# SSD scan slots put into one fixed TensorE order, decay tables built without TensorE, transposes of a tile kept together

## The chip, the cores and the metric

The kernel runs on one core of a Trainium2 chip. The metric is the device time of one launch in microseconds (us). PE is TensorE, DVE is VectorE, ACT is ScalarE, POOL is GpSimd; SP issues nearly all DMAs.

## The reference

Two layers act on 1024 latent tokens and 256 context tokens of width 1024: windowed attention, then a bidirectional Mamba-2 (SSD) mixer, then a final norm. The change lies in the SSD layer, which has 8 groups of 4 heads and cuts the sequence into chunks of 128 tokens:

```python
xbc = jax.nn.silu(centred_depthwise_conv(xbc, conv_w, conv_b))
...
a_cs = jnp.cumsum(da, axis=2)
decay_to_end = jnp.exp(a_last[:, :, None] - a_cs)
states = jnp.einsum('bcsgn,bcsgr,bcsgrp->bcgrpn', bm, decay_to_end, xdt)
...
lmat = jnp.exp(jnp.where(lower, diff, -jnp.inf))
cb = jnp.einsum('bcqgn,bcsgn->bcqsg', cm, bm)
y_diag = jnp.einsum('bcqsg,bcqsgr,bcsgrp->bcqgrp', cb, lmat, xdt)
y_off = jnp.einsum('bcqgn,bcgrpn,bcqgr->bcqgrp', cm, h_prev, jnp.exp(a_cs))
```

Here `diff[q, s] = a_cs[q] - a_cs[s]`. A forward and a backward pass both start from states that the context leaves. The sum of both is gated with `silu(z)`, normalised per group and multiplied by `w_out`.

## The kernel before

All weights and activations of the projections are split into a high and a low fp32r part, and each product is three matmuls (`wh*uH`, `wh*uL`, `wl*uH`).

**Front.** `front` computes for one group, as a generator that yields after each matmul: four tiles of 128 channels (`bT`, two halves of x in `cacc`, `cT`) and the gate `z`. A latent tile is 48 matmuls of 512 columns (L1069) into `pj2` (two buffers); for `bT` and the x halves 24 matmuls of 256 columns (L1060) into `psD` (one buffer) come first for the context. What follows a tile is put into a queue (`Queue`) of small steps: on ACT the conv's middle tap (L982), on DVE four taps (L986), on ACT a tanh (L993), on DVE the silu (L994), then transposes on PE (L1033) back into the same PSUM tile and copies on ACT (L1036). Steps given with a delay come out when so much PE cost has been yielded (`LATE`).

**Chain.** `states` makes, for each group, 11 steps that carry the states through the context and backward through the latent chunks: `xweight` on POOL (L1144), one matmul into `psD` (L1167), `decay` on POOL (L1149), an add on DVE (L1179).

**Slots.** 64 slots, one for each group and chunk (`slot`), each with: scores `pcb` (L1215), the two inter-chunk products `po` (L1217, L1218), the forward state `S` (L1224), the masked diagonal product `yd` (L1244, against the table `M`), and for the slot before two transposes of the finished row (L1272). `M` is exp of a difference of two rows, made by `decays` in two halves: DMAs bring rows of the cumulative sums, ACT casts them (L1195), four fp32r matmuls with one-hot rows spread them over 128 partitions (L1203), DVE takes the backward half where the mask `before` says so (L1204), ACT applies exp (L1205). All these PSUM tiles share the tag `psX` with three buffers. While the slots of group g run, `fill` draws front matmuls of group g+1 (in the last group: matmuls of the output projection, L1484) between them.

**What sets the order.** The code gives a priority order; a scheduler then reorders the instructions of each engine, PE's among them, by what its own model finds ready. Each engine executes its own list in order. Before the slots, `ssd_consts` computes dt, the cumulative sums and their exponentials for all groups (L914 to L976), beside the front of group 0.

Of the kernel before, what the change touches and what calls it, by code (L numbers as in the profile page):

```python
# [17 lines left out]
P = 128  # L18
D = 1024
KT = D // P  # L20
LAT = 1024
# [24 lines left out]
    cacc=2, cctx=1, bT=2, cT=2, xn4=4, xn2=1, bn4=4, bn2=1, sz=2, xw=2, hf=2, hx=2, M=2, y2=1, xs=1, uT=2, pj2=2, psX=3, sk=2, dg=2,  # L46
# [13 lines left out]
LATE = 3.0  # L60
SEGS = (1.5, 2.0, 2.0, 2.2, 2.2)
# [3 lines left out]
class Queue:  # L65
# [10 lines left out]
    def pop(self):  # L76
        if not self.q:
            self.late.popleft()[1]()
            return
        f = self.q.popleft()  # L80
        if isinstance(f, tuple):
            self.late.extend((self.now + f[0], x) for x in f[1])
        else:
            f()
# [19 lines left out]
class Kernel:  # L104
# [758 lines left out]
    def ssd_consts(self, p):  # L863
# [18 lines left out]
        self.dtb = t(p, [P, NCH, 32], F32, "dtb")  # L882
        self.eal = t(p, [P, 64, NT], F32, "eal")

        self.acs_d = t(dr, [2, 64, LAT], F32, "acs")
        self.v_d = t(dr, [2, 64, LAT], F32, "vrow")
# [28 lines left out]
        for lo, n, chunks in ((0, 768, (0, 1, 2, 3, 8, 9)), (768, 512, (4, 5, 6, 7))):  # L915
# [24 lines left out]
            def rows(dst, src):  # L940
                h = t(q, [64, 512], F32R, "rowh", 2)
                l = t(q, [64, 512], F32R, "rowl", 2)
                nc.scalar.copy(h, src[:, :512])
                nc.vector.tensor_sub(l, src[:, :512], h)
                for x, y in enumerate((h, l)):
                    nc.sync.dma_start(dst[x, :, chunks[0] * P : chunks[0] * P + 512], y.bitcast(F32))

            rows(self.acs_d, acs)
# [11 lines left out]
            rows(self.v_d, ln)  # L960
# [6 lines left out]
            for b, c in enumerate(chunks):  # L967
# [4 lines left out]
                if c < NCH:  # L972
# [3 lines left out]
                    nc.scalar.copy(self.dtb[:, c, :], pt[:, 160:192])  # L976
        nc.sync.dma_start(self.eal, eal_d.broadcast_to([P, 64, NT]))
# [12 lines left out]
    def silu(self, raw, acc):  # L990
# [3 lines left out]
                lambda: nc.vector.scalar_tensor_tensor(acc, in0=raw, scalar=1.0, in1=acc, op0=ALU.add, op1=ALU.mult)]  # L994

    def front(self, g, st, post, first=None):
# [31 lines left out]
        def natural(raw, acc, dst, o, n):  # L1028
# [12 lines left out]
            return [(LATE, steps)]  # L1041
# [9 lines left out]
        for n, (x, kind) in enumerate(tiles):  # L1051
# [4 lines left out]
            if nat:  # L1056
                raw = t(ps, [P, 512], F32, "psD")[:, :CTX]
                for k in range(KT):
                    for y, (l, r) in enumerate(((wh, uH), (wh, uL), (wl, uH))):
                        nc.tensor.matmul(raw, l[:, k, :], r[2][:, k, :], start=k + y == 0, stop=k == KT - 1 and y == 2)  # L1060
                        yield N256
                acc = t(pf, [P, CTX], F32, "cctx")
                post.extend(self.taps(x, raw, acc, 0, CTX, CTX) + self.silu(raw, acc) + natural(raw, acc, [(st[nat[0]][2], 0, 2)], nat[1], 2))
# [16 lines left out]
            post.append((LATE, [done]) if nat else done)  # L1080
        need(w)
# [28 lines left out]
    def ssd(self, c0):  # L1110
# [11 lines left out]
        rraw = t(ps2, [32, 6, P], F32, "rraw")  # L1122
        rrow = t(ps2, [P, 6, P], F32R, "rrow")
        nc.sync.dma_start(rraw, a["rrow"].rearrange("p (r n) -> p r n", r=6))
        nc.vector.memset(rrow.bitcast(F32), 0.0)
# [60 lines left out]
        def load_rows(n):  # L1186
            g, c = divmod(n, NCH)
            cs = slice(c * P, (c + 1) * P)
            ar = self.acs_d.rearrange("h (d k) n -> (h d) k n", d=2)[:, 4 * g : 4 * g + 4, cs]
            nc.sync.dma_start(rraw[0:4, :4], ar)  # L1190
            for d in range(2):
                nc.sync.dma_start(rraw[4 + 8 * d : 12 + 8 * d, 4 + d], self.v_d[:, hd(d, g), cs])

        def round_rows(n):
            nc.scalar.copy(rrow[:32], rraw)  # L1195
            if n + 1 < G * NCH:
                load_rows(n + 1)

# [437 lines left out]
```

## Time and profile before

| | us |
|---|---|
| runs | 1855.55, 1860.01, 1861.53; median 1860.01 |
| the profiled execution | 1855.31, of which span 1853.6 |
| SSD slots, first scores to the last diagonal product (starts) | 868.1 to 1752.7 |
| PE busy | 1779.0 of the span |
| DVE / ACT / POOL busy | 1172.0 / 898.8 / 730.7 |

A matmul's row gives a start and a modelled end, and ends overlap the next start; what a matmul costs PE is read from one start to the next.

### The profile page before, as it was taken

The numbers are of one execution on the slowest core, as the hardware profiler recorded it, in microseconds if no ns is written. First come the engines' busy times: TensorE is split into PE (matmuls) and PEld (weight loads), VectorE is DVE, ScalarE is ACT, GpSimd is POOL, SyncE is SP. The second block draws the span as 40 slices with busy tenths as digits, with TensorE's granted clock in tenths as the row PEclk, the third lists the DMA queues.
The fourth block names the chain that finished last, engine by engine and source line by source line (L and its number), as shares of the span: only waits on it lengthen the run. The fifth ranks groups of instructions, "written<-read, shape, count | busy, mean of one in ns | idle before, by whom it ended". The sixth has DMA issues, their size and how long they took to land. (4 is left out here: it accounts for less than half of the span.)

```text
span 1853.6 us, 29612 instructions
## 1 busy us (share of the span) xinstructions
PE 1779.0 (96%) x10628; PEld 1531.0 (83%) x10628; DVE 1172.0 (63%) x2208; ACT 898.8 (48%) x1852; POOL 730.7 (39%) x1007
## 2 busy tenths in 40 slices
PE   6999999999999899879999999999999999999997
PEld 4797767788898787668898898989889898988886
DVE  3654437877778666773766657576665756754743
ACT  3521236777788664652444435344443534543532
POOL 2441137654466465003352443525344352542411
PEclk9999999999999999889999999999999999999998
DMA  8767866443354435121111111111111111433552
GB/s 295 279 168 239 286 166 153 116 107 97 91 135 123 131 122 188 61 64 35 31 46 45 35 46 34 47 33 39 53 34 47 34 48 33 152 114 97 178 162 71
DMA packets 145491, 196.30 MB, mean 106 GB/s; under 512 B 15392, under 2 KB 84896, under 8 KB 144320
## 3 DMA queue, kind: packets, MB, share of 16 engines
q1 hardware_dynamic: 111280, 175.76, 29.6%
q0 software_dynamic: 34064, 18.65, 5.5%
q8 instruction: 84, 1.38, 0.3%
q14 instruction: 63, 0.52, 0.1%
HBM read 158.73 MB, written 35.92 MB: 105 GB/s over the span
## 5 line engine op out<-in xcount | busy, mean ns | idle before, releaser
L222 PE MATMUL pj<-uH,wh 128*128 128x256 f32 (+1 forms) x652 | 232.8, 357 | 7.6 <-DVE rope_b L531 2.3
L224 PE MATMUL pj<-uH,wl 128*128 128x256 f32 (+1 forms) x652 | 219.2, 336 | 0.0
L223 PE MATMUL pj<-uL,wh 128*128 128x256 f32 (+1 forms) x652 | 219.2, 336 | 0.0
L1144 POOL TENSOR_TENSOR xw<-xn,dtdec 128x256 f32<-128x256 f32 x144 | 106.4, 741 | 210.4 <-PE psD L1167 103.1
L1069 PE MATMUL pj<-uH,wh 128*128 128x512 f32 x512 | 172.1, 406 | 1.2 <-ACT xn L1036 1.2
L1069 PE MATMUL pj<-uH,wl 128*128 128x512 f32 x512 | 171.6, 404 | 0.0
L1069 PE MATMUL pj<-uL,wh 128*128 128x512 f32 x512 | 168.2, 398 | 0.0
L210 POOL TENSOR_TENSOR wl<-wr,wh 128x512 fp32r<-128x512 f32 x92 | 121.6, 1325 | 98.3 <-ACT wh L208 97.2
L1094 PE MATMUL pj<-wh,uH 128*128 128x256 f32 x512 | 154.7, 302 | 0.0
L698 DVE TENSOR_TENSOR pl<-pt,ph 128x512 fp32r<-128x512 f32 x168 | 114.3, 688 | 60.7 <-ACT ph L697 59.9
L222 PEld LDWEIGHTS pj<-uH,wh 128*128 128x128 f32 x652 | 123.9, 190 | 34.2 <-issue 7.8
L1094 PE MATMUL pj<-wh,uL 128*128 128x256 f32 x512 | 151.2, 295 | 0.0
L1094 PE MATMUL pj<-wl,uH 128*128 128x256 f32 x512 | 150.8, 295 | 0.0
L1273 ACT ACTIVATE uT<-psX,nw 128x128 f32<-128x128 f32 x128 | 46.9, 367 | 190.1 <-PE psX L1272 189.0
L224 PEld LDWEIGHTS pj<-uH,wl 128*128 128x128 f32 x652 | 123.6, 190 | 14.8 <-issue 1.7
L672 DVE CUSTOM_DVE_ANT_0 sm<-S,mask,nsink 128x640 f32<-128x640 f32 (+2 forms) x160 | 118.8, 772 | 24.6 <-PE S L669 12.2
L208 ACT CAST wh<-wr 128x512 fp32r<-128x512 f32 (+1 forms) x132 | 84.8, 645 | 101.3 <-PE pj L223 74.2
L223 PEld LDWEIGHTS pj<-uL,wh 128*128 128x128 f32 x652 | 124.2, 191 | 11.5 <-issue 2.8
L697 ACT CAST ph<-pt 128x512 fp32r<-128x512 f32 x168 | 97.4, 585 | 63.8 <-PE pt L693 58.4
L674 ACT ACTIVATE sm<-sm,nm 128x640 f32<-128x640 f32 (+2 forms) x160 | 118.5, 742 | 11.7 <-DVE nm L672 11.5
L1239 POOL TENSOR_TENSOR xs<-xn,sk 128x256 f32<-128x256 f32 x64 | 42.0, 656 | 184.8 <-DVE sk L1235 183.6
L1069 PEld LDWEIGHTS pj<-uL,wh 128*128 128x128 f32 x512 | 95.6, 188 | 19.9
(345 smaller groups left out, 5043.4 us busy)
## 6 DMA issues: line engine op xcount, KB each, us to landing
wr<-w_x SPq DMA_DIRECT2D x32, 512.0 KB
wr<-w_sk SPq DMA_DIRECT2D x24, 512.0 KB
wr<-wg SPq DMA_DIRECT2D x44, 256.0 KB
qs<-q POOLq DMA_DIRECT2D x40, 256.0 KB, 3.7
wr<-wo SPq DMA_DIRECT2D x40, 256.0 KB
wada<-w_ad SPq DMA_DIRECT2D x8, 1024.0 KB
wr<-wq SPq DMA_DIRECT2D x32, 256.0 KB
wl<-w_ada SPq DMA_DIRECT2D x32, 256.0 KB
```

Of the source, the lines that this page charges most:

```text
L208: nc.scalar.copy(h, raw)
L210: (eng or nc.vector).tensor_tensor(l, raw, h, op=ALU.subtract)
L222: self.nc.tensor.matmul(ps, lh, rh, start=first and i == 0, stop=False)
L223: self.nc.tensor.matmul(ps, lh, rl, start=False, stop=False)
L224: self.nc.tensor.matmul(ps, ll, rh, start=False, stop=last and i == n - 1)
L672: nc.vector.tensor_tensor_reduce(out=sm[:, :W], in0=Sv, in1=self.mask[:, m0 : m0 + W], scale=-SCALE, scalar=self.nsink[:, 4 * j + r : 4 * ...
L674: nc.scalar.activation(sm[:, :W], sm[:, :W], AF.Exp, bias=nm[:, r : r + 1], scale=-1.0, accum_out=sums[:, r : r + 1])
L697: nc.scalar.copy(ph, ptf)
L698: nc.vector.tensor_sub(pl, ptf, ph)
L1069: nc.tensor.matmul(raw[:, 512 * i : 512 * i + 512], l[:, k, :], r[i][:, k, :], start=k + y == 0, stop=k == KT - 1 and y == 2)
L1094: nc.tensor.matmul(pj[:, c], l, r[:, k, :], start=c % 2 + q + k + y == 0, stop=c % 2 == 1 and q == 1 and k == 3 and y == 2)
L1144: nc.gpsimd.tensor_tensor(xw, X(st, c).rearrange("p (r h) -> p r h", r=R), self.dtdec[:, c, hd(d, g)].unsqueeze(2).broadcast_to([P, R, HP] ...
```

## The change

1. `decays` no longer uses PE. Two DMAs per slot bring the cumulative sums of one direction, broadcast to 128 partitions, into `fd` and `bd` (128x4x128, 256 KB each). POOL adds the offset `vo` to `bd`, DVE copies `bd` into `fd` where `before` says so, ACT applies exp with the bias `vf` in four instructions of 128 columns, and `fd` is then `M`. The offsets come from one more transpose per chunk in `ssd_consts`; the fp32r split of the rows (`rows`) and `round_rows` go. `fd` and `bd` have two buffers each. The new `decays` of the next slot is held behind the DVE gate product and POOL's power of this one.
2. `slot` is cut into `diagonal`, `finish`, `scores`, `state`, `inter` and written out software-pipelined, with new shares of front work between (`SEGS`). `pin` chains every PE instruction of groups 0 to 6 to the one before, so that PE keeps the order of the code there.
3. In `front`, the latent matmuls of a tile come before its context matmuls; all transposes of a tile come before all its copies; the delays are 12 for the latent transposes (they were 3) and 7.5 for the context's.
4. The chain's steps are drawn in `run` by the cost spent, not three per slot.

```diff
-LATE = 3.0
-SEGS = (1.5, 2.0, 2.0, 2.2, 2.2)
+LATE = 12.0
+BD = 2
+SEGS = (2.6, 2.4, 2.2, 2.25)
...
-            rows(self.acs_d, acs)
+            nc.sync.dma_start(self.acs_d[0][:, chunks[0] * P : chunks[0] * P + 512], acs[:, :512])
...
-            rows(self.v_d, ln)
...
+                    nc.tensor.transpose(pt[:, 192:256], ln[:, sl], self.ident[:64, :64])
+                    nc.scalar.copy(self.vf[:, c, :], pt[:, 192:224])
+                    nc.vector.tensor_sub(self.vo[:, c, :], pt[:, 224:256], self.vf[:, c, :])
...
+    def pin(self, first):
+        traced = self.nc.cur_bb.bb.instructions
+        start = next(k for k in reversed(range(len(traced))) if traced[k] is first) + 1
+        last = None
+        for i in traced[start:]:
+            if i.engine == mybir.EngineType.PE:
+                if last is not None:
+                    self.tc.add_manual_dep(i, last.name, mybir.DependencyInfo(mybir.DependencyClass.NoSync, mybir.DependencyReason.DATA), reason="pin")
+                last = i
...
-            return [(LATE, steps)]
+            return [(late, steps[::2] + steps[1::2])]
...
-        def decays(n, M, half):
-            o = t(ps, [P, 512], F32, "psX").rearrange("p (d r n) -> p d r n", d=2, r=2)
-            for d in range(2):
-                nc.tensor.matmul(o[:, d], rrow[:, 4 + d], rrow[:, 2 * half : 2 * half + 2], start=True, stop=True)
-            nc.vector.copy_predicated(o[:, 0], self.before.unsqueeze(1).broadcast_to([P, 2, P]), o[:, 1])
-            nc.scalar.activation(M[:, 2 * half : 2 * half + 2], o[:, 0], AF.Exp)
+        def decays(n):
+            g, c = divmod(n, NCH)
+            x, y = [rows.pop((n, d)) for d in range(2)]
+            nc.gpsimd.tensor_tensor(y, y, self.vo[:, c, 4 * g : 4 * g + 4].unsqueeze(2).broadcast_to([P, R, P]), op=ALU.add)
+            nc.vector.copy_predicated(x, self.before.unsqueeze(1).broadcast_to([P, R, P]), y)
+            for r in range(R):
+                nc.scalar.activation(x[:, r], x[:, r], AF.Exp, bias=self.vf[:, c, 4 * g + r : 4 * g + r + 1])
+            load_rows(n + BD, 1)
+            return x
...
+                    ss, ymul, pw = diagonal(n, st, cur)
+                    if tail:
+                        tail()
+                    load_rows(n + 2, 0)
+                    if n + 1 < G * NCH:
+                        with self.tc.issue_after(ymul), self.tc.issue_after(pw):
+                            cur = {"M": decays(n + 1)}
+                    tail = finish(n, ss)
+                    fill(0)
...
+                    scores(n + 1, st, cur)
+                    fill(1)
+                    if c < NCH - 1:
+                        fs = state(n + 1, st, cur)
+                        next(fs)
+                        inter(n + 1, st, cur)
+                        fill(2)
+                        for _ in fs:
+                            pass
```

**Where PE's list changes inside a slot.** Group 1, the diagonal product of the third chunk, before: `psX` from `M` is that product, `rrow` the table for the next slot, `y` a finished row, `cacc` a silu'd latent tile and `cctx` a context one that go back transposed.

```order
L1244 MATMUL psX_11091<-xn_2278_9683,M_10970 128x64 x4
L1272 MATMUL psX_11096<-ident_63,y_2190_8955 128x128
L1033 MATMUL pj_2519_11028<-ident_63,cacc_11029 128x128 x4
L1069 MATMUL pj_2553_11230<-uH_2039_8207,wh_11112 128x512
L1069 MATMUL pj_2553_11230<-uH_2126_8627,wh_11112 128x512
L1069 MATMUL pj_2553_11230<-uL_2040_8208,wh_11112 128x512
L1203 MATMUL psX_11117<-rrow_8950 128x256 x2
L1069 MATMUL pj_2553_11230<-uL_2127_8628,wh_11112 128x512
L1033 MATMUL psD_10987<-ident_63,cctx_11027 128x128 x2
```

And of the change, the same group, between the third chunk's diagonal product and the next scores (L1214): the last of 11 latent matmuls that follow the product and the finished row's two transposes, then the context's transposes.

```order
L1068 MATMUL pj_2503_10946<-uH_2039_8207,wh_10845 128x512
L1068 MATMUL pj_2503_10946<-uH_2126_8627,wh_10845 128x512
L1068 MATMUL pj_2503_10946<-uL_2040_8208,wh_10845 128x512
L1068 MATMUL pj_2503_10946<-uL_2127_8628,wh_10845 128x512
L1040 MATMUL psD_10902<-ident_63,cctx_10943 128x128 x2
L1214 MATMUL psX_11038<-cT_10234,bT_9714 128x128
```

The `rrow` matmuls are gone, and the place of the context's transposes is fixed: 24 context and 34 latent matmuls behind the end of the latent tile of `bT`, and the slots' own between, whatever DVE has done by then.

**What DVE has to do before those transposes.** The change's DVE list in that stretch, up to the silu of `cctx` (L990) for which they wait; ahead of it stand the gate product L1261, two taps of `bT` with the new masked copy L1204 between, the weight split L1020, a first tap of `cctx` and `y2` (L1232).

```order
L982 SCALAR_TENSOR_TENSOR bT_10796<-pj_2477_10795,cw_8675,bT_10796 128x1023
L1216 TENSOR_TENSOR fd_10776<-fd_10776,psX_10919 128x512
L1219 ISA xs_10922,dg_10923<-psX_10919,ident_63 128x128
L1219 ISA dg_10923 128x1
L982 SCALAR_TENSOR_TENSOR cctx_10943<-psD_10902,cw_8675,cctx_10943 128x255
L1248 TENSOR_TENSOR hf_10961<-hf_10961,psX_10960 128x256
L982 SCALAR_TENSOR_TENSOR bT_10796<-pj_2477_10795,cw_8675,bT_10796 128x1022
L1221 SCALAR_TENSOR_TENSOR sk_10925<-dtb_8689,dg_10923,dsk_8683 128x4
L982 SCALAR_TENSOR_TENSOR cctx_10943<-psD_10902,cw_8675,cctx_10943 128x255
L982 SCALAR_TENSOR_TENSOR cctx_10943<-psD_10902,cw_8675,cctx_10943 128x254
L990 SCALAR_TENSOR_TENSOR bT_10796<-pj_2477_10795,bT_10796 128x1024
L990 SCALAR_TENSOR_TENSOR cctx_10943<-psD_10902,cctx_10943 128x256
```

The latent tile's taps and silu now stand among those of the context tile, because both matmul blocks end within a few us of each other.

**Where the slots begin.** The change's PE list as the front of group 0 ends; `psD` from `xw` are steps of the chain (L1173), `pj` from `uH` the front of group 1.

```order
L1104 MATMUL pj_2245_9512<-wh_9372,uL_2127_8628 128x256
L1214 MATMUL psX_9661<-cT_9286,bT_8979 128x128
L1173 MATMUL psD_9540<-xw_9517,bn_2190_8968 128x256
L1173 MATMUL psD_9561<-xw_9538,bn_2189_8967 128x256
L1173 MATMUL psD_9582<-xw_9559,bn_2189_8967 128x256
L1173 MATMUL psD_9607<-xw_9580,bn_2189_8967 128x256
L1247 MATMUL psX_9672<-xw_9670,bn_2189_8967 128x256
L1229 MATMUL psX_9677<-hf_2231_9413,cT_9286 128x256
L1256 MATMUL psX_9684<-xn_2186_8964,fd_8956 128x64 x4
L1068 MATMUL pj_2285_9713<-uH_2039_8207,wh_9594 128x512
```

Four steps of the chain stand one behind the other with no front matmul between; before, 21 latent matmuls of group 1 (L1069) stood between two of its last steps.

More of the change, by code (lines that the diff above doesn't have):

```diff
@@ L1055, in front @@
             wh, wl = cur["h"], cur["l"]
[L1056 to L1063, printed above, removed]
             raw = t(ps, [P, LAT], F32, "pj2")
@@ L1307, in ssd @@
                 else:
+                    self.pin(first)
                     cf.close()
```

211 lines of the change are left out of this document (107 added, 104 removed).

## The prediction

> **What bounds the kernel now.** I read the page's shares first, then the busy time by stretch, then PE's timeline inside the slots.
>
> ```profile
> span 1853.6 us, 29612 instructions
> PE 1779.0 (96%) x10628; PEld 1531.0 (83%) x10628; DVE 1172.0 (63%) x2208; ACT 898.8 (48%) x1852; POOL 730.7 (39%) x1007
> ```
>
> PE is the bound of the whole, but a share of the span says nothing of a stage. So by stretch (columns: stretch, its length, busy us of PE, PEld, DVE, ACT, POOL, granted clock, DMA share, GB/s):
>
> ```profile
> 900.00:1600.00 700.00, 696.57 (x4392) 628.76 (x4391) 464.19 (x851) 311.45 (x637) 277.92 (x419) 1.00 0.16 46
> 1600.00:1750.00 150.00, 148.56 (x802) 127.47 (x801) 93.32 (x165) 70.51 (x138) 62.03 (x79) 1.00 0.40 125
> ```
>
> In the slots PE is busy 99.5% at full clock (0.16 of the DMA engines is used): there an instruction taken from PE shortens the run, and any wait of PE lengthens it. Does PE wait at all there? Its timeline has this wait in a group, between the first scores of groups 2 and 3; the group's row in the view by line follows:
>
> ```profile
> 1157.91 0.70 PE L1167 MATMUL psD<-xw,bn 128*128 128x256 f32 x2 [0.49 <-POOL xw L1144]
> L1167 PE MATMUL psD<-xw,bn 128*128 128x256 f32 x176 | 54.1, 389 | 3.7 <-POOL xw L1144 3.7
> 1087.83 0.38 PE L1215 MATMUL psX<-cT,bT 128*128 128x128 f32 x2
> 1196.40 0.38 PE L1215 MATMUL psX<-cT,bT 128*128 128x128 f32 x2
> ```
>
> A group takes 108.6 us from scores to scores, and 0.49 of it is a wait at the chain's first step. The row by line gives 3.7 us in all: 0.31 once ahead of the slots and 0.49 in each of the seven groups that draw a front. The timeline shows no other wait of PE above 0.05 us in these groups, so nearly all of a period is work.
>
> **The change part by part.** All terms are set against the profiled execution, 1855.3 us.
>
> *PE work removed.* The four spreading matmuls of a slot:
>
> ```profile
> 931.17 0.40 PE L1203 MATMUL psX<-rrow 128*128 128x256 f32 x2
> 931.41 0.39 PE L1069 MATMUL pj<-uL,wh 128*128 128x512 f32 x1
> L1203 PE MATMUL psX<-rrow 128*128 128x256 f32 x256 | 53.5, 290 | 0.0
> ```
>
> Two of them cost 0.24 from start to start; 256 cost **-30.7**. The 290 ns mean is latency and overlaps. The last group's slots draw the output projection and are not pinned, but PE is busy 148.56 of 150 us there too, so its share (3.8) counts in full.
>
> *PE work added.* Eight 64-row transposes beside the dt work, which cost 0.11 each by the next rows: **+0.9**.
>
> ```profile
> 797.85 0.36 PE L973 MATMUL psX<-ident,w 64*128 64x64 f32 x1 [6.72 <-ACT dtdec L971]
> 798.01 0.31 PE L974 MATMUL psX<-ident,dt 64*128 64x64 f32 x1
> 798.12 0.31 PE L973 MATMUL psX<-ident,w 64*128 64x64 f32 x1
> ```
>
> The 6.72 us wait there is for the dt arithmetic. Four ACT casts and four DVE subtractions go from it, but `bT`'s taps and silu now stand beside it and its transposes behind; I take 0, with -6 to +4.
>
> *The wait of 0.49* goes with the new spacing of the chain: **-3.4** for seven groups.
>
> *What the fixed order costs.* Before, the scheduler put a tile's transposes wherever they were ready:
>
> ```profile
> 1104.10 0.28 PE L1060 MATMUL psD<-uH,wl 128*128 128x256 f32 x1
> 1112.87 0.42 DVE L994 SCALAR_TENSOR_TENSOR cctx<-psD,cctx 128x256 f32<-128x256 f32 x1
> 1117.04 0.39 PE L1033 MATMUL psD<-ident,cctx 128*128 128x128 f32 x2
> 907.38 0.59 PE L1217 MATMUL psX<-hf,cT 128*128 128x256 f32 x2
> 907.81 0.59 PE L1218 MATMUL psX<-hb,cT 128*128 128x256 f32 x2
> ```
>
> The silu ended 8.9 us after the context matmuls, the transposes came at 12.7. In the new order they come 10.0 behind them. For the first tile I count from the end of `bT`'s latent matmuls. PE has 24 context matmuls of 0.12, 34 latent of 0.23, and 2.6 of slot work (a 256-column fp32 product is 0.43 by the last two rows): 13.2 us. DVE's list in that stretch goes by these rows:
>
> ```profile
> L986 DVE SCALAR_TENSOR_TENSOR bT<-pj,cw,bT 128x1022 f32<-128x1022 f32 x12 | 15.3, 1278 | 19.7 <-ACT bT L982 19.7
> L994 DVE SCALAR_TENSOR_TENSOR bT<-pj,bT 128x1024 f32<-128x1024 f32 x6 | 7.3, 1213 | 0.0
> L986 DVE SCALAR_TENSOR_TENSOR cctx<-psD,cw,cctx 128x254 f32<-128x254 f32 x40 | 19.0, 475 | 0.2
> L1013 DVE TENSOR_TENSOR wl<-wr,wh 128x1024 fp32r<-128x1024 f32 x39 | 48.3, 1239 | 0.2
> L1219 DVE TENSOR_TENSOR M<-M,psX 128x512 f32<-128x512 f32 x52 | 35.6, 684 | 34.2 <-PE psX L1215 31.5 <-ACT M L1205 2.7
> L1204 DVE COPY_PREDICATED psX<-before,psX 128x256 f32<-128x256 int32 x104 | 44.0, 424 | 54.1 <-PE psX L1203 53.5
> L982 ACT ACTIVATE bT<-pj,cb,cw 128x1024 f32<-128x1024 f32 x6 | 7.2, 1207 | 69.5 <-PE pj L1069 69.5
> L993 ACT ACTIVATE pj<-bT 128x1024 f32<-128x1024 f32 x6 | 6.2, 1030 | 3.5 <-DVE bT L986 3.5
> ```
>
> ACT's tap opens it at 1.6 us. Then 4 taps and the silu of `bT` (6.3), the same of `cctx` (2.3), the split (1.2), `y2` and the product with `M` (0.7 each), 1.0 of small ones (an add of 0.42 and three shorter) and 0.7 for the wider masked copy: 12.9 us in 19 instructions, less 1.5 because each starts some 0.08 before the last one's end, plus 0.9 of waiting for `bT`'s tanh. DVE is done at 14.1, so PE waits 0.9. Walked the same way, DVE is done 9.5 behind the second tile's context matmuls, where the order allows 9.7, and 10.7 behind the third's, where it allows 10.0. That is 0 and 0.7: 1.6 a group, **+11.2** over seven. Bounds: 0 (DVE as quick as the 8.9 above) and 5 a group (two more such waits at diagonal products and a slower DVE).
>
> *Where the slots begin* four chain steps stand without filler. A step's loop is the matmul, DVE's add and POOL's two products:
>
> ```profile
> 845.02 0.59 PE L1167 MATMUL psD<-xw,bn 128*128 128x256 f32 x2
> 845.72 0.42 DVE L1179 TENSOR_TENSOR hf<-hf,psD 128x256 f32<-128x256 f32 x1 [1.77 <-PE psD L1167]
> 846.27 0.62 POOL L1149 TENSOR_TENSOR hf<-hf,eal 128x256 f32<-128x256 f32 x1
> ```
>
> Some 1.3 us a step, of which PE works 0.43: four cost **+3.5** once, 0 to 8.
>
> *What is hidden.* The new `M` runs POOL power, POOL add, masked copy, exp, product:
>
> ```profile
> L210 POOL TENSOR_TENSOR wl<-wr,wh 128x512 fp32r<-128x512 f32 x92 | 121.6, 1325 | 98.3 <-ACT wh L208 97.2
> L1256 POOL TENSOR_TENSOR ss<-ss,half 128x1 f32<-128x1 f32 x52 | 29.5, 568 | 117.1 <-ACT y L1255 117.1
> L1252 DVE TENSOR_TENSOR y<-y,psX 128x256 f32<-128x256 f32 x52 | 21.7, 417 | 35.7 <-PE psX L1244 15.8 <-POOL y L1241 14.7 <-PE psX L1272 5.1
> L1253 DVE TENSOR_TENSOR y<-y,sz 128x256 f32<-128x256 f32 x52 | 23.8, 457 | 0.6
> L1255 ACT ACTIVATE y<-y 128x257 f32<-128x257 f32 x52 | 21.8, 418 | 19.6 <-DVE y L1253 19.6
> L1273 ACT ACTIVATE uT<-psX,nw 128x128 f32<-128x128 f32 x104 | 38.2, 368 | 173.0 <-PE psX L1272 172.0
> L1144 POOL TENSOR_TENSOR xw<-xn,dtdec x144: 607/613/1613, 839.5 to 1702.4; 128x256 f32<-128x256 f32 x144
> ```
>
> The trace has no such POOL add; a 128x512 subtraction took 1.33, twice the quickest half-size product is 1.21; I take 1.33. The masked copy in SBUF lies between 0.42 (half as wide) and twice that; I take 0.7 after the 0.68 product. Four exps are 1.5. So a table is ready, from the start of the diagonal product before it, after that product (0.9, eight records of 0.11), DVE's add and gate (0.9), ACT's square with its sum (0.6), the power (0.6), the add (1.3), the copy (0.7), the exps (1.5) and the product with `M` (0.7): 7.2, and some 8 with eight handovers of 0.1. By the costs of the instructions between them the products stand 11.9 to 14.4 apart, so PE's own work covers it where DVE's 1.2 us taps do not queue ahead at each of its three steps, and what queues behind the held POOL add (chain products of 0.6) has that slack too. POOL rises from 278 to some 350 of 700 us. The loads of `fd` and `bd` are 33 MB more over 870 us on DMA engines 16% used, asked for two slots ahead; SP may stand at the `fd` load until the diagonal product ends, and the weights behind it are due a tile later. ACT gains the cast and pays the split exps; the net is near nothing.
>
> Sum: -30.7 + 0.9 - 3.4 + 11.2 + 3.5 = -18.5, so 1836.8. The median of the runs shown lies 4.7 above the profiled one; I give 1839 for a median.
>
> **The rivals.**
>
> *No waits:* DVE keeps the 8.9 us seen, the order costs PE nothing, 1825.6 with the 3.5 at the start. Against it: the latent taps now fall among the context's. Chance 0.20.
>
> *It gives back what it takes:* waits of 4 us a group, 1854. For it: PE can no longer run past a late tile. Against: the walk finds 1.6. Chance 0.09.
>
> *Slower, by the table's chain:* POOL and DVE get in each other's way, so every table comes 2 us later. For it: the same POOL product takes 613 ns in the median and 1613 at worst, and the chain crosses POOL twice. My walk leaves 1.0 to 2.4 us at three diagonal products; at a spare of 1.2, 2 us more make PE wait 0.8 at 56 slots: 1825.6 + 45 = 1871. It decides from 1.7 us more a table on. Against: most POOL rows are at the median. Chance 0.11. The Trainium skill, "SBUF — State Buffer", section "SBUF: two separate sides", speaks for this one: a DVE operation with two SBUF inputs and a GpSimd operation exclude each other for a whole instruction, and the masked copy now has two. By that rule each table could lose one POOL add, 1.33 us, which stays under the 1.7; the 613 against 1613 ns agrees that something blocks POOL at times.
>
> **How the numbers follow.** My forecast (1829 to 1848) has 0.60. The range 1821 to 1858 takes in most of the first rival and the second, and leaves out the slower one and the lowest of the first, under 0.2. A measurement can tell 0.3%, 5.6 us, from no change. Faster 0.80 (0.60 + 0.20), same 0.09, slower 0.11.
>
> **What would show it.** The removed work: a group's period of 103.8 us plus 0.5 plus its waits, 105.9 by the forecast. The order's cost: PE idle ahead of the context's transposes (first and third tile), released by DVE's silu. The start: idle PE between the last chain steps before slot 0. The slower rival: PE idle ahead of diagonal products, released by DVE's product with `M`, and longer POOL rows. It is wrong if idle time shows at each slot, or if a group takes over 108.

## The result, and the profile after

| | before | after |
|---|---|---|
| median of 4 runs, us | 1858.59 (1855.55 to 1861.53) | 1843.04 (1842.35 to 1845.01) |
| ratio of the times | 1 | 0.9918, 95% interval 0.9899 to 0.9937 |
| the profiled execution, of which span | 1855.31, 1853.6 | 1845.01, 1843.3 |
| a group's period, scores to scores | 108.6 | 105.5 |
| PE waiting in such a period | 0.49 | 0.97 |
| last group's first scores to the end of the output projection | 157.2 | 167.2 |

The changed kernel is 0.8% faster, and the whole interval lies beyond the 0.3% that a measurement can tell from no change. One run of the experiment with transposes and copies in turn (3204.3, granted clock 0.80) and one of the kernel before beside the five mends (1984.8, 0.84) were slow, and medians and ratios here leave them out. The page's first lines and the same two stretches as before (columns: stretch, length, busy us of PE, PEld, DVE, ACT, POOL, granted clock, DMA share, GB/s):

```profile
span 1843.3 us, 29181 instructions
PE 1759.6 (95%) x10380; PEld 1504.9 (82%) x10380; DVE 1179.0 (64%) x2147; ACT 884.9 (48%) x1918; POOL 806.6 (44%) x1071
```

```profile
900.00:1600.00 700.00, 693.01 (x4293) 618.94 (x4292) 480.93 (x825) 312.13 (x703) 347.91 (x488) 1.00 0.32 86
1600.00:1750.00 150.00, 145.56 (x754) 123.64 (x753) 97.83 (x151) 70.00 (x145) 68.71 (x75) 1.00 0.54 162
```

The instruction count of PE falls by 248: 256 spreading matmuls gone, 8 transposes come. POOL takes the 348 of 700 us that were reckoned with, and the DMA share doubles to 0.32. In the slots PE is still busy 99%, so a period is still nearly all PE work. The table's last row grows by 10 us mostly because work has moved: 57 gate matmuls of group 7's front (0.12 us each, 6.8 in all) and 12 matmuls of the output projection (0.23 each, 2.8), which stood ahead of the last group's first scores, now stand behind them. The timeline gives the period and its waits (columns: start, length, engine, line, operation, and in brackets PE's wait and who ended it):

```profile
1083.29 0.38 PE L1214 MATMUL psX<-cT,bT 128*128 128x128 f32 x2
1121.77 0.44 PE L1040 MATMUL psD<-ident,cctx 128*128 128x128 f32 x2 [0.71 <-DVE cctx L990]
1160.13 0.44 PE L1040 MATMUL psD<-ident,cctx 128*128 128x128 f32 x2 [0.26 <-DVE cctx L990]
1188.77 0.38 PE L1214 MATMUL psX<-cT,bT 128*128 128x128 f32 x2
```

From 1083.29 to 1188.77 is 105.48. PE waits for DVE's silu ahead of the context's transposes of the first and the third tile, as forecast, and at no other place of a group for more than 0.06 us. A bracket counts from the modelled end of the matmul ahead; from start to start the two waits cost 0.87 and 0.42. The chain's wait of 0.49 is gone. Two places outside the steady groups were not forecast so. The first is where the slots begin:

```profile
870.30 0.70 PE L1173 MATMUL psD<-xw,bn 128*128 128x256 f32 x2
871.59 0.70 PE L1173 MATMUL psD<-xw,bn 128*128 128x256 f32 x2 [0.59 <-DVE hb L1185]
872.92 1.21 DVE L1020 TENSOR_TENSOR wl<-wr,wh 128x1024 fp32r<-128x1024 f32 x1
873.08 1.53 POOL L1223 TENSOR_TENSOR xs<-xn,sk 128x256 f32<-128x256 f32 x1
874.06 0.41 DVE L1185 TENSOR_TENSOR hb<-hb,psD 128x256 f32<-128x256 f32 x1
874.52 1.22 PE L1173 MATMUL psD<-xw,bn 128*128 128x256 f32 x2 [2.23 <-DVE hb L1185]
```

```profile
869.80:874.50 4.70, 1.77 (x8) 0.78 (x6) 4.64 (x9) 1.96 (x2) 4.42 (x6) 1.00 0.00 0
874.50:884.70 10.20, 9.60 (x27) 7.48 (x27) 1.26 (x3) 0.00 (x0) 3.67 (x7) 0.50 0.27 75
884.70:900.00 15.30, 15.30 (x87) 13.35 (x86) 7.69 (x14) 5.17 (x14) 7.70 (x11) 1.00 0.21 41
```

The four unfilled chain steps leave PE idle for 3.5 us, 2.23 of it because DVE's add (L1185) stands behind the front's weight split (L1020). Then the granted clock is 0.50 for 10.2 us: a chain step that elsewhere takes 0.59 takes 1.22. Half of 10.2 is some 5.1 us of work lost, more than the idle time itself. The second place is the last group, which draws the output projection (L1524):

```profile
1617.73 0.50 PE L1524 MATMUL pj<-uH,wh 128*128 128x512 f32 x1 [1.15 <-ACT wh L1456]
1619.93 0.50 PE L1524 MATMUL pj<-uH,wl 128*128 128x512 f32 x1 [1.47 <-DVE wl L1460]
...
1622.61 0.47 PE L1104 MATMUL pj<-wl,uH 128*128 128x256 f32 x1
...
1630.49 0.50 PE L1524 MATMUL pj<-uH,wh 128*128 128x512 f32 x1 [1.11 <-ACT wh L1456]
```

The scheduler put 12 projection matmuls ahead of the last gate matmuls (L1104), where their weights were not yet split. PE waits 4.7 us from the last group's first scores to the matmul behind the projection, against 1.4 before.

### The profile page after: what moved, and what is told of

The parts are those of the page before. It is cut to its first block, busy times and chain, and to the rows that moved or that the text cites. A ratio compares the mean times of both kernels' runs of the same rounds, so it can differ in the third digit from the quotient of the medians.

```text
span 1843.3 us, 29181 instructions
## 1 busy us (share of the span) xinstructions
PE 1759.6 (95%) x10380; PEld 1504.9 (82%) x10380; DVE 1179.0 (64%) x2147; ACT 884.9 (48%) x1918; POOL 806.6 (44%) x1071
## 5 line engine op out<-in xcount | busy, mean ns | idle before, releaser
L1068 PE MATMUL pj<-uH,wl 128*128 128x512 f32 x512 | 175.7, 410 | 0.0
L1068 PE MATMUL pj<-uL,wh 128*128 128x512 f32 x512 | 175.1, 412 | 0.0
L1104 PE MATMUL pj<-wl,uH 128*128 128x256 f32 x512 | 161.0, 314 | 0.0
L1104 PE MATMUL pj<-wh,uH 128*128 128x256 f32 x512 | 149.2, 291 | 1.5 <-ACT xn L1043 1.5
L1104 PE MATMUL pj<-wh,uL 128*128 128x256 f32 x512 | 147.4, 288 | 0.0
L1150 POOL TENSOR_TENSOR xw<-xn,dtdec 128x256 f32<-128x256 f32 x144 | 94.2, 659 | 71.5 <-PE psD L1173 51.6
L1264 POOL TENSOR_TENSOR ss<-ss,half 128x1 f32<-128x1 f32 x64 | 39.5, 617 | 177.4 <-ACT y L1263 176.5
L1235 POOL TENSOR_TENSOR y<-y 128x256 f32<-128x256 f32 x64 | 57.7, 902 | 127.5 <-DVE y L1232 127.5
```

The source lines that it names most:

```text
L1068: nc.tensor.matmul(raw[:, 512 * i : 512 * i + 512], l[:, k, :], r[i][:, k, :], start=k + y == 0, stop=k == KT - 1 and y == 2)
L1104: nc.tensor.matmul(pj[:, c], l, r[:, k, :], start=c % 2 + q + k + y == 0, stop=c % 2 == 1 and q == 1 and k == 3 and y == 2)
L1150: nc.gpsimd.tensor_tensor(xw, X(st, c).rearrange("p (r h) -> p r h", r=R), self.dtdec[:, c, hd(d, g)].unsqueeze(2).broadcast_to([P, R, HP] ...
```

## The experiments

All twelve are edits of the changed kernel, one thing each except the three, four and five mends, timed beside the kernel before on the same chip. Their times are set against the changed kernel's 1843.0, their traces against its 1843.3.

| run | median, us | ratio to before, 95% interval | period of a steady group |
|---|---|---|---|
| PE work put back | 1862.8 | 1.0022 (1.001 to 1.0035) | 108.2 |
| PE's order free | 1868.9 | 1.0055 (1.004 to 1.007) | 108.2 |
| context's transposes 2 us later | 1841.1 | 0.99 (0.9882 to 0.9918) | 105.4 |
| order from the first chain on | 1836.7 | 0.9881 (0.9861 to 0.9901) | 105.5 |
| table 2.1 us later | 1878.8 | 1.0118 (1.0096 to 1.0141) | 110.3 |
| transposes and copies in turn | 1861.9 | 1.0022 (1.0007 to 1.0036) | 108.1 |
| context ahead of latent | 1909.5 | 1.0283 (1.0265 to 1.0301) | 116.1 |
| three mends | 1838.2 | 0.9908 (0.9879 to 0.9937) | 105.0 |
| order over the last group | 1849.8 | 0.9957 (0.9941 to 0.9973) | 105.5 |
| table not held | 2026.9 | 1.0911 (1.0883 to 1.094) | 130 to 136 |
| four mends | 1834.0 | 0.9879 (0.9858 to 0.99) | 105.0 |
| five mends | 1830.6 | 0.9864 (0.9838 to 0.989) | 105.0 |

### PE work put back

```diff
+            if n < (G - 1) * NCH:
+                for _ in range(4):
+                    nc.tensor.matmul(yd[:, 256:], self.uH[0][:, 0, :P], self.uH[0][:, 0, :256], start=True, stop=True)
```

> Puts PE work back and nothing else: in the slots of groups 0 to 6 the diagonal product's PSUM bank gets four more fp32r matmuls of 128x256 (as many per slot, and of the shape, that the spreading ones had), into columns that nobody reads. Theory (PE is the bound of each slot, the removed matmuls were worth 0.12 us each): 224 x 0.12 = 26.9 us more than the changed kernel's 1843.0, so 1870, slower than before by 0.6%; a group's period 105.5 + 3.8 = 109.3. Rival (the gain came from elsewhere, the order or the decays' own path, and PE had waits that such matmuls fill): under 10 us more, 1843 to 1853, period under 107.

Measured: 19.7 us more than the changed kernel. The theory's mechanism holds and its sum does not, as a period shows:

```profile
1193.59 0.38 PE L1214 MATMUL psX<-cT,bT 128*128 128x128 f32 x2
1301.83 0.38 PE L1214 MATMUL psX<-cT,bT 128*128 128x128 f32 x2
```

108.24 is 2.76 above 105.48, and no wait is left in it: the 0.97 ahead of the context's transposes has been filled. From start to start the four matmuls of a slot cost 0.53 (the first 0.20, the others 0.12), 4.25 a group, and the starts at the two former waits lie 1.4 closer together, where the brackets said 0.97. Seven times 2.76 are 19.3. At the 0.12 of most of them the removed matmuls were worth some 30 us over eight groups. The first 1.4 us or so of PE work put into a group are free, as the rival had it, and what goes beyond costs its full time: PE is the bound of the slots.

### PE's order free

```diff
-                    self.pin(first)
```

> Takes away the fixed order alone: the scheduler may reorder PE in groups 0 to 6 again, the rest of the change stays. Theory (the order costs what the trace shows ahead of the context's transposes, 0.71 + 0.25 a group, 6.7 us in seven groups, and brings nothing that the other parts don't): 1836, period 104.5 in steady groups, no wait of PE ahead of the context's transposes. Rival (the order is what keeps the table and the context transposes out of PE's way; free, PE meets operands that are late by the scheduler's model): 1848 or more, with waits at diagonal products or chain steps.

Measured: 25.9 more, the rival's side; without the fixed order the changed kernel is slower than the one before. The waits ahead of the context's transposes do go, and these take their place, in group 6:

```profile
1532.06 0.74 PE L1068 MATMUL pj<-uH,wh 128*128 128x512 f32 x2 [1.32 <-DVE sz L1115]
1546.29 0.70 PE L1247 MATMUL psX<-xw,bn 128*128 128x256 f32 x2 [0.75 <-POOL xw L1150]
1549.85 0.49 PE L1214 MATMUL psX<-cT,bT 128*128 128x128 f32 x2 [0.72 <-ACT uT L1279]
...
1638.26 0.70 PE L1173 MATMUL psD<-xw,bn 128*128 128x256 f32 x2 [1.96 <-DVE hb L1185]
1641.58 1.22 PE L1173 MATMUL psD<-xw,bn 128*128 128x256 f32 x2 [2.62 <-DVE hb L1185]
```

The first three stand in groups 3 to 6 alike: a buffer not yet released by the gate's product, a state product whose `xw` is late, scores that wait for the finished row's copy. With 0.16 at a diagonal product they make 2.95 a group. The last two are part of 8.8 us of waits where group 6 ends. So the order is no price paid for other gains; it is what keeps them.

### The context's transposes later

```diff
-natural(raw2, acc2, [(st[nat[0]][2], 0, 2)], nat[1], 2, 7.5)
+natural(raw2, acc2, [(st[nat[0]][2], 0, 2)], nat[1], 2, 9.5)
-                    post.append((7.5, [lambda: st.setdefault("ctx", True)]))
+                    post.append((9.5, [lambda: st.setdefault("ctx", True)]))
```

> The context's transposes are put 2 us of front work later (delay 9.5 where the change has 7.5), nothing else. Theory (they wait 0.71 and 0.25 a group for DVE's silu, because the order puts them too early): both waits go, 0.96 x 7 = 6.7 us less, 1836, period 104.5. Rival 1 (the chain, which starts behind them, or the next context matmuls, which need their PSUM bank, are late in their place): 1841 to 1845, period 105.3 to 105.7, new waits at chain steps or context matmuls.

Measured: 2 us less, inside the scatter; the rival. The waits named are gone, and one of the same size stands where the chain, which starts 2 us later too, has a step left over:

```profile
1088.35 0.70 PE L1173 MATMUL psD<-xw,bn 128*128 128x256 f32 x2 [1.08 <-POOL xw L1150]
```

### The order from the first chain on

```diff
                 chain = states(0, st)
                 mark = done
+                first = nc.cur_bb.bb.instructions[-1]
```

> The fixed order begins where the chain of group 0 begins, so the chain's steps stand 15 gate matmuls apart inside the front and none is left over where the slots begin. First scores to second scores of group 0 take 16.0 us in the changed kernel, of which 6.8 is work at full clock. Theory (idle PE is followed by some 10 us at half the granted clock, 0.50 from 874.5 to 884.7, so the four steps cost some 3.5 of idle time and 5.1 of clock): with the idle time the half clock goes too, 7 to 9 us less, 1835. Rival 1 (the half clock comes from something else, as the number of steps done since the dt stage): the idle time goes and the clock stays, 3.5 less, 1839.5. Rival 2 (the steps wait inside the front instead): under 2 less.

Measured: 6.3 less in the median, 8.0 in the span. The first group's period falls from 108.0 to 97.3 (that also holds the steps moved ahead of its first scores), and in the place of the half clock the stretch reads:

```profile
878.00:886.00 8.00, 8.00 (x43) 6.77 (x42) 3.52 (x9) 2.93 (x10) 4.24 (x7) 1.00 0.17 48
```

Take the idle time away and the clock stays at 1.00. So the half clock belonged to the idle time, and rival 1, 3.5 us alone, is out by the span and by the clock.

### The table 2.1 us later

```diff
+            for op in (ALU.subtract, ALU.add):
+                nc.gpsimd.tensor_tensor(y, y, self.vo[:, c, 4 * g : 4 * g + 4].unsqueeze(2).broadcast_to([P, R, P]), op=op)
```

> Each table's POOL addition is followed by a subtraction and an addition of the same offset, two more POOL operations of 128x512 (1.04 us each in the changed kernel's trace), so every table comes some 2.1 us later; nothing else. Theory A (the prediction's slower rival: 1.7 us decide, the spare is 1.2 at most slots): PE waits 0.9 at 56 diagonal products, about 50 more, 1893. Theory B (the changed kernel's trace: the exps end 2.8 to 6.3 us behind the scores, and the diagonal product comes 8.4 to 10.4 behind them, so 2.6 to 6 are left after DVE's 0.7): no wait at diagonal products, 1843 to 1847, more only where POOL's chain products behind the longer table come late (0.5 a group, 3.5).

Measured: 35.8 more, between the two and nearer to A. Diagonal products (L1258 here) now wait for DVE's product with `M`; the two largest waits of a group:

```profile
1099.53 1.08 PE L1258 MATMUL psX<-xn,fd 128*128 128x64 f32 x8 [1.00 <-DVE fd L1218]
1164.94 1.08 PE L1258 MATMUL psX<-xn,fd 128*128 128x64 f32 x8 [0.76 <-DVE fd L1218]
```

Five of eight products wait, 3.15 in all, so at those the spare was 1.1 to 1.9 and at the other three over 2.1. Theory B read too much spare off the trace: it counted from the exps, and the product with `M` has its own queue on DVE. With the waits at the other places a group has 3.8 of them, 2.8 more; beside the changed kernel's trace, which has PE's matmuls in the same order, all of the 4.8 us that its period grew lies at these places, in the starts just behind them, and in a few starts that come up to 0.2 late and show no bracket. From start to start a wait costs more than its bracket: 1.16 more than without it where the bracket says 1.00.

### Transposes and copies in turn

```diff
-            return [(late, steps[::2] + steps[1::2])]
+            return [(late, steps)]
```

> Undoes one part: a tile's transposes and its copies are issued in turn again (transpose four, copy, transpose four, copy), with the fixed order as it is. Theory (the second four write the other half of the PSUM tile and need not wait for the first copy; the grouping is worth nothing here): 1843 within 2, period 105.5. Rival (in the fixed order the second transposes stand behind ACT's copy of the first, or the copies hold up ACT's list): a wait of 0.6 to 1 at each of three latent tiles, 12 to 21 more, 1855 to 1864.

Measured: 18.9 more; the rival. One of three such waits in a group:

```profile
1124.02 0.66 PE L1040 MATMUL pj<-ident,bT 128*128 128x128 f32 x4 [0.67 <-ACT bn L1043]
```

The second four transposes wait for ACT's copy of the first four, though they write the other half of the tile. The bracket says 0.67 or 0.68 at each; from start to start each costs 0.84, and the three are 2.5 of the 2.66 that a period grew. This part, which the prediction gave no term, is worth as much as two thirds of the removed matmuls once PE's order is fixed.

### Context ahead of latent

The block of the context's matmuls stands ahead of the latent block again, unchanged.

> Undoes one part: a tile's context matmuls stand ahead of its latent matmuls again, the fixed order and the delays stay. Theory (the waits ahead of the context's transposes come from the latent taps that stand among the context's on DVE; with the context first DVE has only the context's taps there): 0.96 x 7 = 6.7 less, 1836, period 104.5. Rival (the third tile's latent transposes, 12 behind, now come last, so the chain, which needs them, is squeezed into the end of a group and into the place where the slots begin): 1850 or more, waits at chain steps.

Measured: 66.5 more. The theory is out, and the rival had the sign and not the place. PE's timeline in group 2, with the last DVE instruction before it:

```profile
1187.53 1.22 DVE L990 SCALAR_TENSOR_TENSOR cT<-pj,cT 128x1024 f32<-128x1024 f32 x1 [1.15 <-ACT pj L989]
1188.90 0.55 PE L1103 MATMUL pj<-wh,uH 128*128 128x256 f32 x1 [10.27 <-DVE cT L990]
...
1191.39 1.45 PE L1040 MATMUL pj<-ident,cacc 128*128 128x128 f32 x8
```

The first gate matmul needs one of the two latent PSUM buffers. The third tile's transposes, which free one, are placed 12 us of front work behind their taps; without the 24 context matmuls only the 11 us of `cT`'s matmuls stand before the gate; so the gate waits for the other, until DVE has done all taps and the silu of `cT`. 10.27 in each of seven groups, less 0.97, is 65. That this is close to 66.5 is partly chance: a period grew by 10.6, with the clock still at 0.50 when the gate starts, some 72 in seven groups, and the stretches ahead of the first scores and in the last group came out 6.7 shorter.

### Three mends

```diff
+                elif i == 1 and q == 0:
+                    st["next"] = weights(a["w_sk"][0, 0], 2, 512)
+                    post.extend(st["next"]["steps"])
...
-nat[1], 2, 7.5)
+nat[1], 2, 9.5 if kind == "bT" else 7.5)
```

with the edit of the order's start, and `ssd_out` taking that first weight.

> Three mends of the changed kernel at once: the fixed order begins with the chain of group 0 (8 less in the profile before this, 6.3 in the median); the context's transposes of the first tile alone stand 2 us later (0.71 x 7 = 5.0 less, the chain's start untouched, so without the wait of 1.08 at a chain step that the delay of all three brought); the output projection's first weights are loaded and split behind the last group's gate weights (two waits of 1.15 and 1.47 go, 2.6 less). Theory (each is where the trace puts it and they add): 1843.0 - 6.3 - 5.0 - 2.6 = 1829, period 104.8. Rival (each wait taken away comes back a few instructions later): 1834 to 1837, period 105.2 or more.

Measured: 4.9 less than the changed kernel, and no less than the order's start alone; 9 above the sum and 1 above the rival's range. In its trace the first scores come at 873.4; in that of the four mends, which execute the same up to there, at 869.6, so 3.8 of the shortfall are scatter ahead of the slots. The first tile's wait fell to 0.23 and the period to 105.0. The weights split early changed nothing, for the projection's matmuls still stood ahead of the gate's:

```profile
1607.35 0.50 PE L1525 MATMUL pj<-uH,wh 128*128 128x512 f32 x1 [1.56 <-ACT wh L1016]
1609.10 0.50 PE L1525 MATMUL pj<-uH,wl 128*128 128x512 f32 x1 [1.03 <-DVE wl L1020]
```

### The order over the last group

```diff
-                    self.pin(first)
...
                 if g < G - 1:
                     run(1e9)
+            self.pin(first)
```

> Extends the fixed order over the last group's slots, which draw the output projection; nothing else. In the changed kernel the scheduler put the first 12 output matmuls ahead of the last gate matmuls of group 7's front, where their weights were not split yet: waits of 1.15, 1.47 and 1.11 ahead of them, 4.4 in all from there to the end of the projection, where the kernel before has 1.4. Theory (the last group's gain of 3.8 went into these waits, because PE's list there was the scheduler's): in the code's order the gate matmuls come first and cover the split; 2.5 to 3.5 less, 1840. Rival (the weights are late wherever the projection starts, or the fixed order makes new waits at the output rows, as a free order did not): 1843 or more.

Measured: no gain but 6.7 more, 1849.8, the rival. Its profiled execution has the changed kernel's span (1843.4); its other runs are slower with a granted clock of 0.979 to 0.983, where the changed kernel's have 0.982 to 0.986. The waits at the projection are down from 4.2 to 1.4 and a new one stands at the last chain step:

```profile
1618.05 1.22 PE L1173 MATMUL psD<-xw,bn 128*128 128x256 f32 x2 [3.98 <-DVE hb L1185]
```

### The table not held

```diff
-                        with self.tc.issue_after(ymul), self.tc.issue_after(pw):
-                            cur = {"M": decays(n + 1)}
+                        cur = {"M": decays(n + 1)}
```

> Undoes one part: the POOL addition, the masked copy and the exps of the next table are no longer held behind the gate product on DVE and the power on POOL, so the scheduler may put them earlier or later on those engines; PE's order stays. Theory (the table has 2.6 to 6 to spare at each diagonal product, so its place matters little): 1843 within 3, period 105.5. Rival (held behind them, the addition and the copy keep out of the way of the finished row's own chain; free, they stand ahead of it, the row comes late and its two transposes make PE wait): waits ahead of the row's transposes or the scores, 0.3 or more a slot, 1860 or more.

Measured: 183.9 more, by far the largest. Who waited for whom (columns: total us, times, longest), and the loads' row (times issued, size, us from issue to landing):

```profile
POOL bd L1203 <- DMA bd<-acs: 215.9, 48, 13.1
...
DVE fd L1204 <- DMA fd<-acs: 145.9, 56, 6.2
...
PE psD L1040 <- DVE cctx L990: 90.0, 22, 6.2
```

```profile
fd<-acs SPq DMA_DIRECT2D x64, 256.0 KB, 4.8
```

In the changed kernel DVE's masked copy waited once for `fd`, 2.3 us, and POOL's addition never for `bd`; the load took the same 4.8 us there. What changed is the place of the table's instructions: the scheduler put them a slot earlier in POOL's and DVE's lists, ahead of a load that cannot begin before the diagonal product two slots back has freed its buffer. What follows them in those lists, the taps and the chain's products, stood too, and PE waited 17 to 21 us a group, most of it ahead of the context's transposes; over groups 1 to 4 its granted clock averaged 0.90 to 0.93. Both theories were wrong: the hold keeps the table behind its load, not behind the finished row.

### Four mends, five mends

The four are the three and the order over the last group. For the fifth:

```diff
+                def high():
+                    with self.tc.issue_after(hold()[0]):
+                        nc.scalar.copy(hi, feats[n])
+                def late():
+                    with self.tc.issue_after(hold()[1]):
+                        low()
-                post.extend([lambda: nc.scalar.copy(hi, feats[n]), low])
+                post.extend([high, late] if 6 <= n < 10 else [lambda: nc.scalar.copy(hi, feats[n]), low])
```

where `hold()` gives the newest slot's square on ACT and gate product on DVE.

> The three mends of the run before (fixed order from the chain of group 0 on, first tile's context transposes 2 us later, output weights split behind the last gate weights) and the fixed order over the last group as well. The third of them alone did nothing (waits of 1.56, 1.03 and 1.12 stayed), since the projection's first matmuls still stood ahead of the gate's. Theory (their place was the cause): those go too, 3.5 to 4 less than the three mends' profile of 1837, 1833. Rival (as the run beside it): no less than 1836.

> The four mends, and one more: in the last group the splits of the 7th to 10th output feature tile are held behind a finished row's square on ACT and gate product on DVE. In the runs with the order fixed over the last group PE waits 3.97 at the last chain step of group 7; DVE's add before it stands behind two feature splits and the projection's first weight split, and ACT's square and weight cast stand behind a feature cast that waited 4.72 for its load. Theory (these casts in ACT's and DVE's lists are the cause): the wait falls under 0.5 and the half clock behind it (chain step 1.06 where 0.59 is usual) goes too, 4 to 5.5 less than the run before it, 1829. Rival (the wait moves to the projection's own matmuls, which now get their features late): 1832 to 1836.

Measured, the four: 1834.0, the theory's time, but not by its cause. The last group's first scores to the end of the projection took 170.1 where the three mends took 168.8, and PE's waits there, counted to the matmul behind it, rose from 4.7 to 6.0; the gain lies ahead of the first scores (3.8) and behind the projection (1.5), where the two versions execute the same; the second is the clock's, as the last section shows. By the place of the waits the rival holds. ACT and PE at the end of group 7's chain:

```profile
1600.66 0.62 ACT L1484 CAST uH<-oraw 128x512 fp32r<-128x512 f32 x1 [4.72 <-DMA oraw<-uN]
1602.26 1.04 ACT L1016 CAST wh<-wr 128x1024 fp32r<-128x1024 f32 x1
1605.90 1.06 PE L1176 MATMUL psD<-xw,bn 128*128 128x256 f32 x2 [3.97 <-DVE hb L1188]
```

Measured, the five: 1830.6, and at the same chain step:

```profile
1603.75 0.70 PE L1176 MATMUL psD<-xw,bn 128*128 128x256 f32 x2 [0.18 <-DVE hb L1188]
```

A feature cast that waited 4.72 for its load held up ACT's list, through it DVE's add, and so PE. Put behind, the wait falls to 0.18, and the last group's first scores to the end of the projection take 164.4 where they took 170.1, a little over the 4 to 5.5 expected; the span fell by 2.6 only, since the stretches before and behind came out 1.6 and 1.5 longer, where the two versions execute the same. This version beats both kernels: 0.9864 of the time before, where the change has 0.9918. The medians say nothing of the fifth mend alone: the kernel before took 1853.8 beside it and 1857.4 beside the four, and the intervals of the two ratios overlap; that it removes the wait stands on the traces.

## Why the prediction was right, point by point

The forecast was 1839 and 1843.0 was measured, in the range; the sum against the profiled execution was -18.5 and the profile shows -10.3. The median came nearer than the sum by luck: the profiled execution was 3.3 below the median before, and 2.0 above it after the change.

- **PE work removed**, -30.7: right. Put back, three of every four such matmuls cost the 0.12 reckoned with.
- **The wait of 0.49**, -3.4: right, gone in all seven groups.
- **The dt stage**, 0: right within its bounds. Its waits of 0.97 and 5.87 stand where 6.72 stood.
- **What the fixed order costs**, +11.2: mechanism right (PE ahead of the context's transposes, first and third tile, released by DVE's silu), size a little too large. Forecast 0.9, 0 and 0.7; measured 0.71, 0 and 0.26 in the brackets, 7.0 in all, and from start to start 0.87, 0 and 0.42, 9.2 in all. The forecast's terms for the first tile (1.6 + 12.9 - 1.5 + 0.9) add up to 13.9 and not 14.1, so its wait should have read 0.7 and the whole +9.8. But as a judgement of the order the step was one-sided: it priced what the order takes and took for granted that a free order would meet no late operands, since it did not in the kernel before. With the other parts changed, a free order costs 25.9.
- **Where the slots begin**, +3.5: right as idle time, 3.53. What follows it, 5.1 us of half clock, had no term, though the trace of before showed the like:

```profile
797.80:806.00 8.20, 7.79 (x41) 6.90 (x42) 8.02 (x10) 6.68 (x29) 0.00 (x0) 0.51 0.28 76
```

  This follows the 6.72 of waiting at 797.85. A wait of PE should have been priced with the clock behind it, though how long that lasts is partly chance: behind the same waits at this place it was 10.2 us again with PE work put back, but 6.8 with the context's transposes later and with the order over the last group.
- **"Its share (3.8) counts in full"** in the last group: this failed. PE was busy there before, but its order there is the scheduler's, and it put the projection's matmuls ahead of their weights: 4.7 of waits where 1.4 were, so 3.3 of the 3.8 went. The run with the order over that group moved the wait to a chain step, and holding back the feature casts then removed it.
- **What is hidden**, the new table: right, no diagonal product waits. The addition took 1.04 (1.33 taken), the masked copy 0.74 (0.7 taken). It is hidden by little and only in its place: 2.1 us later costs 36, and not held it costs 184.

Together, with the waits by their brackets: -30.7 + 0.9 - 3.4 + 7.0 + 3.5 + 5.1 + 3.3 is -14.3 against -10.3. From start to start the order's waits are 2.2 more and the seven waits of 0.49 some 1 more, so about 3 us were not traced. The terms that failed, +5.1 and +3.3, were in small part paid by the one that was too large.

Of the rivals, "no waits" fell to the 0.97 a group. "It gives back what it takes" had waits of 4 a group, which the trace does not show. The slower one did not occur, but its price was of the right size, 45 us for a table 2 us late where 2.1 us cost 35.8: it put 1.2 of spare at a slot, and five of eight slots have 1.1 to 1.9. The additions all took their own time (64 rows, shortest, median and longest):

```profile
L1203 POOL TENSOR_TENSOR bd<-bd,vo x64: 1029/1039/1124, 836.9 to 1706.0; 128x512 f32<-128x512 f32 x64
L1204 DVE COPY_PREDICATED fd<-before,bd x64: 723/740/1270, 838.0 to 1707.6; 128x512 f32<-128x512 int32 x64
L1223 POOL TENSOR_TENSOR xs<-xn,sk x64: 603/613/1682, 873.1 to 1712.3; 128x256 f32<-128x256 f32 x64
```

The Trainium skill's rule, cited there from "SBUF — State Buffer", section "SBUF: two separate sides", agrees with single rows: POOL's `xs` at 873.08 took 1.53 where 0.61 is usual and ended 0.48 behind DVE's weight split, and copies took up to 1.27 where 0.74 is usual. No addition was lengthened by more than 0.1, so by these rows a table lost at most 0.6.

## What to carry to other kernels

When PE is the bound, take the removed work at its start-to-start cost, and then ask for each place where the order changes what PE meets there that is late: the parts of this change that had no price (an order fixed, transposes grouped, one block behind another, a table held behind another instruction) are worth 19 to 184 us each, against 30 for the matmuls. An instruction whose load cannot begin until a buffer is free belongs in its engine's list behind that moment, or it holds up all that follows. Price a wait of PE with the slow clock behind it, and look for the scheduler's own choices where a hand-written order ends.

## What the runs showed of the hardware

- **Short waits halve the clock, and for longer than they last.** After 0.59 and 2.23 us of waiting with one chain step between, PE had 0.50 for 10.2 us, though it was busy for most of that time. After 3.97 us, in the four mends, 0.53 for 3.6 us:

```profile
1605.90:1609.50 3.60, 3.60 (x11) 2.97 (x11) 2.23 (x6) 1.28 (x4) 2.79 (x4) 0.53 0.63 192
```

  And after 1.15 and 1.47 us at 1617.73 and 1619.93 in the changed kernel it stayed 1.00. The Trainium skill, "TensorE: Matmul & The Clock Gate", section "Part 1: The HAM clock gate", gives an idle window of some 3.4 us for the fall to half clock and as much sustained work for the return; here 2.8 us in two pieces sufficed, and the return took 3.4 us in one case and 10.2 in another.
- **How a wait falls between fixed moments decides whether the clock drops.** In each of the fourteen traces the clock changes only at moments whole steps of 3.413 us apart: in the changed kernel half clock begins at 795.97, 840.34 and 874.47, which are 13 and 10 steps apart, and within the runs it lasts 3.4, 6.8, 10.2 or 13.7 us. Between 200 us and the last 15 us of the spans, a step at full clock with up to 1.39 us of waits (by their brackets) was never followed by half clock, one with 1.91 or more always was, and between the two both occur. Behind the projection all versions have the same wait, of 1.91 to 2.04 us. In the three mends (the first two rows) it falls into one step, in the four mends (the others) across two:

```profile
1780.63:1784.04 3.41, 1.50 (x13) 1.31 (x12) 3.41 (x7) 1.47 (x3) 0.00 (x0) 1.00 1.03 390
1784.04:1787.45 3.41, 3.41 (x18) 3.41 (x18) 1.01 (x1) 0.39 (x1) 2.15 (x2) 0.50 0.94 309
1776.77:1780.18 3.41, 2.49 (x21) 2.27 (x19) 3.41 (x6) 1.00 (x1) 0.00 (x0) 1.00 0.88 329
1780.18:1783.59 3.41, 2.42 (x20) 2.45 (x21) 2.37 (x4) 0.85 (x3) 1.92 (x2) 1.00 1.01 382
```

  The stretch from the projection's end to the span's end takes 66.7 us in the first and 65.2 in the second. So a microsecond or two between two traces can be chance. Why half clock then lasts one step or three, no run here shows.
- **Equal programs differ by the clock.** Up to the slots the run with PE work put back executes what the changed kernel does, yet its first scores came at 866.3 and not 869.8; up to there it had half clock for 30.7 us and the changed kernel for 44.4. Groups 1 to 5 of a run repeat to 0.3 us, except with PE's order free and with the table not held.
